# Transposing 256 tokens instead of all 1040 before the first projections of a hybrid attention and convolution block

## The chip, the core and the metric

The kernel is one program on one core of a Trainium2 chip. Its time is the device time of one execution in microseconds (us), and a lower time is better. Of the engines, PE multiplies matrices (PEld is its loading of weights), DVE is the vector engine, ACT the scalar engine, POOL the general one, and SP issues most of the loads and stores (DMA). Each engine works through its own list of instructions in order: where an instruction waits, all that is behind it on that engine waits too. SBUF is the on-chip memory, PSUM the banks into which PE adds up its products.

## The reference, cut to what is computed

```python
n = _rms(h, norm_mix_w[l])                 # h: 1040 tokens (16 meta, 1024 positions) x 1024 features
z = n @ w_in[l]                            # 7168 columns
q, k, v, glu, g_att, g_conv = jnp.split(z, splits, axis=-1)
o = _diff_attention(q, k, v, lam, cid)     # 8 heads, two maps each, block-causal
y_att = (_rms(o, subln_w[l]) * (1.0 - lambda_init)).reshape(b, lp, ATT_V)
u = glu[..., :CONV_CH] * jax.nn.sigmoid(glu[..., CONV_CH:])
u = jax.nn.silu(_layernorm(_causal_dwconv(u, ...), ...))      # 31 taps
m = jax.nn.sigmoid(g_att) * y_att + jax.nn.sigmoid(g_conv) * (u @ w_conv_out[l])
h = h + m @ w_out[l]
up = _causal_dwconv(_rms(h, norm_ffn_w[l]) @ w_up[l], ...)    # 3 taps
h = h + (silu(gate) * val) @ w_down[l]
out = _rms(h, norm_final_w)
```

`_rms(x, w)` divides each token by the root of its mean square over the 1024 features and multiplies by `w`. The matrix products are float32, made of three products of two rounded parts each (`hi hi`, `lo hi`, `hi lo`).

## The kernel before, in words

The products want the features on the 128 partitions: `xh` and `xl`, [128, 8 feature tiles, 1040 tokens], hold the two parts of the normalised tokens. The input comes in both layouts, `x` by tokens and `xT` feature-major, but the start of the kernel reads `x` alone. In three groups of 384, 384 and 272 tokens (the loop over `gi`), tiles `xt` of 128 tokens are loaded; ACT squares each with a sum along the row (L213), POOL turns the sum into a root (L214, L215), DVE scales the tile by it (L216), PE transposes it feature tile by feature tile into a pair of PSUM banks `ps_x` (L222), ACT writes `xh` from there (L225) and DVE `xl` (L226). 18 products `warm` of ones (L186) run on PE before the first tokens are there.

A weight's column tile [128, 1024] is loaded one use ahead and parted by ACT and DVE (`load_w`, L118 and L119). `mm3` (L143 to L145) is the three products of one feature tile; a "pass" below is the 24 products of one weight and one chunk of tokens.

Eight steps follow, one for each head (`inputs`). A step makes, for the three chunks of `CH_ALL`, the two halves of the gated unit (`ps_b`, through tanh on ACT into `tb`, then `ps_a`, which DVE multiplies into `u`, L278), then a gate (`ps_g`), the key (`ps_k`), the query (`ps_q`) and the value (`ps_v`); gate and query go by `CH_OUT`, chunks of 342. These use two PSUM banks in turn (`bank`). Step 0 makes the key of a chunk right behind its `ps_b` and `ps_a`. Beside the products of step i runs the attention of head i-1 (`attention`), a unit of work for each half pass, in the order of the table `UNITS`: `s` are scores, `v` turns the values, `t` turns the probabilities, `a` multiplies them with the values, and `n` (`norm`, L553 to L556) divides the outputs of the head before by their root mean square. Scores, `norm` and `ps_x` share two PSUM pairs (tag "s") in turn; `norm` holds its pair `ps_ss` until DVE has multiplied `os` by it (L556). A step begins with the units `s0 v0 n`, `s1`, (empty), `v1`, `s2`; so the pair that `norm` holds is the one that `s2` gets. The convolution runs on DVE with the lowest priority. The order on each engine is set by a scheduler that knows priorities and its own guess of durations, and then stands fixed in the program.

After the eight steps come the remaining gates, the merge and output projection, and a gated MLP; the change doesn't touch their code.

Of the kernel before, what the change touches and what calls it, by code (L numbers as in the profile page):

```python
# [19 lines left out]
KT = 8                # feature tiles of the model width  # L20
WARM = 18
T = 1040              # 16 meta tokens and 1024 positions
NM = 16               # meta tokens
T0 = 14               # first token whose residual stream is needed
TN = T - T0           # 1026
# [4 lines left out]
FT = 22               # feature tiles of the gate (and of the value)  # L30
LAMBDA_INIT = 0.2
CH_ALL = [(0, 348), (348, 346), (694, 346)]
CH_OUT = [(14, 342), (356, 342), (698, 342)]
NEG = -1e30
# A head's attention by units of work: v by tokens, scores, transposes, products with v, and the norm of the
# head before it.  A unit goes with half a bank of another product's passes.
# [15 lines left out]
LATE = 7                # the first head whose gate is computed after the last step  # L52
STATS_FROM, METAS_FROM = 8, 18          # units of the last head's attention
LATER = 1000            # what gives way: the convolution to the next step's work, a chunk's last scaling to the
                        # next chunk's sums
DIRECT = 2              # of w_up's tiles, pairs by plain products
W_LATER = 300           # the parts of a weight that is not used yet
GROUPS = [3, 4, 4]      # pairs of feature tiles that w_down's products sum over in PSUM
AHEAD, BEFORE = 5, 3    # steps whose parts are made ahead, and those of them before the last tile of w_up is done
# [3 lines left out]
def trunk_kernel(  # L63
    ctx: ExitStack,
    tc: tile.TileContext,
    x: bass.AP,         # [1040, 1024]     meta tokens and positions
    xT: bass.AP,        # [128, 8, 1040]   the same, feature-major
    w_in: bass.AP,      # [56, 128, 1024]  per column tile: [k within tile, (k tile, column)]
    w_co: bass.AP,      # [8, 128, 1024]
    w_o: bass.AP,       # [8, 128, 1024]  # L70
    w_up: bass.AP,      # [44, 128, 1024]
    w_dn: bass.AP,      # [22, 128, 1024]  rows of w_down
    lam4: bass.AP,      # [128, 4, 64]
    pvec: bass.AP,      # [128, 49]  norm_mix, norm_ffn, norm_final, ln_w, ln_b, dw_b (8 each), subln
    dww: bass.AP,       # [128, 8, 31]
    fdw: bass.AP,       # [128, 44, 3]
    fdb: bass.AP,       # [128, 44]
    out: bass.AP,       # [128, 8, 1024]
):
    nc = tc.nc  # L80
    # ------------------------------------------------------------ constants
# [28 lines left out]
    def load_w(src, later):  # L110
        """Column tile of a weight as its two float32r parts."""
        raw = wpool.tile([P, KT * P], F32, tag="wraw", name="wraw", bufs=2)
# [10 lines left out]
    class Weights:  # L123
        """The column tiles in the order of their use, each loaded one use ahead."""
# [4 lines left out]
        def ahead(self):  # L129
            if self.srcs:  # L130
                self.ready.append(load_w(self.srcs.pop(0), self.later))
# [9 lines left out]
    def mm3(ps, lh, ll, rh, rl, start, stop):  # L141
        """ps += l^T r from the two parts of each operand."""
        nc.tensor.matmul(ps, lh, rh, start=start, stop=False)  # L143
        nc.tensor.matmul(ps, lh, rl, start=False, stop=False)  # L144
        nc.tensor.matmul(ps, ll, rh, start=False, stop=stop)  # L145
# [13 lines left out]
    def rstd(dst, src, eps, n):  # L159
        """dst = (src / n + eps) ** -0.5"""  # L160
        nc.scalar.activation(dst, src, AF.Ln, bias=eps, scale=1.0 / n)
        nc.scalar.activation(dst, dst, AF.Exp, scale=-0.5)

    # =================================================== phase A: mixing inputs
# [18 lines left out]
    # ---- the tensor engine's clock rises while the first tokens arrive  # L183
# [4 lines left out]
    # ---- normalised tokens, transposed  # L188
# [8 lines left out]
    with tc.tile_pool(name="xp", bufs=2, reuse_waits="tile") as xp:  # L197
        rt = xp.tile([P, 9], F32, tag="rt", name="rt", bufs=1)
        nc.sync.dma_start(pv, pvec)
        for gi, (o, n) in enumerate(((0, 384), (384, 384), (768, 272))):  # L200
            tiles = []
            for t in range(o, o + n, P):
                r = min(P, T - t)
                xt = xp.tile([P, D], F32, tag="xt", name="xt", bufs=6)
                nc.sync.dma_start(xt[:r], x[t:t + r, :])
                tiles.append((t, r, xt))
            if gi == 0:
                for _ in range(3):
                    weights.ahead()
            for t, r, xt in tiles:  # L210
                c = rt[:r, t // P:t // P + 1]
                sq = xp.tile([P, D], F32, tag="sq", name="sq", bufs=2)
                nc.scalar.activation(sq[:r], xt[:r], AF.Square, accum_out=c)  # L213
                nc.gpsimd.tensor_scalar(c, c, 1.0 / D, 1e-6, op0=ALU.mult, op1=ALU.add)  # L214
                nc.gpsimd.tensor_tensor(out=c, in0=c, in1=half[:r], op=ALU.pow)  # L215
                nc.vector.tensor_scalar(xt[:r], xt[:r], c, None, op0=ALU.mult)  # L216
            for k in range(KT):
                if k % 2 == 0:
                    ps = ps_s.tile([P, 2, 512], F32, tag="s", name="ps_x")
                xn = ps[:, k % 2, :]  # L220
                for t, r, xt in tiles:
                    nc.tensor.transpose(xn[:, t - o:t - o + r], xt[:r, P * k:P * k + P], ident[:r, :r])  # L222
                xn = xn[:, :n]
                nw = pv[:, k:k + 1]
# [988 lines left out]
```

## Time and profile before

| | us |
|---|---|
| time, median of 3 runs | 1747.07 |
| lowest and highest | 1746.29, 1747.51 |
| span of the profiled execution | 1740.7 |
| until the first product of the gate of step 0 | 62.70 |
| PE busy in that stretch | 54.43 |
| PE busy from there to 740 | 677.30 of 677.30 |

The profiled execution has 1740.7 us from its first to its last instruction, 6.4 us less than the median time. In the profile a group of instructions is named by its line in the code, its engine, its operation and by "out<-in" with the names of tiles; "idle before" is what the engine waited ahead of it, and the arrow names what released it.

### The profile page before, as it was taken

To read this page: it belongs to the slowest core of one execution; us is meant where nothing else is said; L and a number is where in the kernel's file an instruction comes from. 1 tells how busy PE (TensorE), PEld (TensorE's weight loads), DVE (VectorE), ACT (ScalarE), POOL (GpSimd) and SP (SyncE) were. 2 spreads that over 40 slices of the span, in tenths; PEclk is the share of its full clock that TensorE was granted. 3 is DMA by queue.
4 is the path that set the end of the run, shared out by engine and by line. 5 is a ranking of instruction groups with operands and counts; after the bars stand their busy time and mean duration, and the time that the engine had idled before them with its cause. 6 is when DMAs were issued, how large, how long until landed. Compare 5 with 4: busy or idle time off the path is not lost.

```text
span 1740.7 us, 29030 instructions
## 1 busy us (share of the span) xinstructions
PE 1716.3 (99%) x11736; PEld 1651.5 (95%) x11736; DVE 1391.4 (80%) x2065; ACT 849.6 (49%) x1407; POOL 39.4 (2%) x75
## 2 busy tenths in 40 slices
PE   8999999999999999999999999999999999999997
PEld 6999999999999999998999999999999999988886
DVE  5679697978888797986357466998888888799997
ACT  6245565646464637565642245543334434353345
POOL 2020000000000000000000000000000000000010
PEclk9999999999999999999999999999999999999999
DMA  4323222141414141367648443322222221583622
GB/s 167 98 67 86 79 66 88 54 111 50 116 49 105 49 111 42 104 193 221 183 136 250 170 144 112 121 98 79 80 74 73 86 85 37 188 279 100 189 55 97
DMA packets 80710, 195.58 MB, mean 112 GB/s; under 512 B 8624, under 2 KB 26416, under 8 KB 80192
## 3 DMA queue, kind: packets, MB, share of 16 engines
q1 hardware_dynamic: 78416, 187.43, 33.8%
q0 software_dynamic: 2160, 6.29, 2.0%
q8 instruction: 92, 1.51, 0.4%
q14 instruction: 42, 0.34, 0.1%
HBM read 130.54 MB, written 40.93 MB: 99 GB/s over the span
## 4 chain that ended last, share of the span: by engine, by line
PE 89%; DMA 5%; DVE 3%; ACT 1%; issue 1%; SPq 0%; POOL 0%; DVEq 0%; ACTq 0%
PE ps_u L144 8%; PE ps_u L145 8%; PE ps_u L143 8%; PE ps_d L145 4%; PE ps_d L143 4%; PE ps_d L144 4%; PE ps_g L143 3%; PE ps_g L144 3%; PE ps_g L145 3%; PE ps_s L398 2%; PE ps_s L399 2%; PE pt L508 2%; PE ps_o L143 2%; PE ps_o L144 2%; PE ps_o L145 2%; PE ps_b L144 2%
## 5 line engine op out<-in xcount | busy, mean ns | idle before, releaser
L299 DVE SCALAR_TENSOR_TENSOR acc<-d,taps,acc 128x513 f32<-128x513 f32 x248 | 170.3, 746 | 0.5
L118 ACT CAST whi<-wraw 128x1024 fp32r<-128x1024 f32 x84 | 88.1, 1050 | 119.5 <-PE ps_o L144 31.4
L145 PE MATMUL ps_g<-xh,wlo 128*128 128x342 f32 x384 | 125.6, 327 | 0.0
L143 PE MATMUL ps_g<-xh,whi 128*128 128x342 f32 x384 | 124.9, 325 | 0.5 <-ACT tg L264 0.5
L143 PE MATMUL ps_d<-part 128*128 128x512 f32 (+1 forms) x324 | 123.9, 382 | 0.0
L144 PE MATMUL ps_d<-part 128*128 128x512 f32 (+1 forms) x324 | 122.8, 379 | 0.9 <-DVE part L981 0.9
L144 PE MATMUL ps_g<-xl,whi 128*128 128x342 f32 x384 | 123.7, 322 | 0.0
L145 PE MATMUL ps_d<-part 128*128 128x512 f32 (+1 forms) x324 | 123.4, 381 | 0.0
L926 DVE TENSOR_TENSOR u<-ps_u,u 128x516 f32<-128x516 f32 x140 | 94.7, 689 | 34.8 <-PE ps_u L145 34.3
L119 DVE TENSOR_TENSOR wlo<-wraw,whi 128x1024 fp32r<-128x1024 f32 x84 | 102.3, 1218 | 22.0 <-ACT whi L118 20.2
L1009 ACT CAST part<-raw 128x1024 fp32r<-128x1024 f32 x66 | 69.0, 1051 | 95.0 <-PE ps_d L145 73.9
L827 DVE SCALAR_TENSOR_TENSOR g<-u,fw,g 128x1024 f32<-128x1024 f32 x88 | 110.6, 1277 | 0.6
L299 DVE SCALAR_TENSOR_TENSOR acc<-u,tab,acc 128x513 f32<-128x513 f32 x120 | 88.5, 737 | 0.8
L981 DVE TENSOR_TENSOR part<-raw,part 128x1024 fp32r<-128x1024 f32 x66 | 80.0, 1218 | 5.0 <-ACT part L1009 4.4
L143 PEld LDWEIGHTS ps_g<-xh,whi 128*128 128x128 f32 x384 | 73.0, 190 | 1.2 <-ACT tg L264 0.8
L144 PEld LDWEIGHTS ps_d<-part 128*128 128x128 f32 x324 | 60.9, 188 | 13.6 <-DVE part L981 1.4
L143 PE MATMUL ps_o<-mmh,whi 128*128 128x258 f32 x256 | 72.5, 283 | 1.0 <-DVE sg L744 1.0
L145 PEld LDWEIGHTS ps_g<-xh,wlo 128*128 128x128 f32 x384 | 72.9, 190 | 0.3
L144 PEld LDWEIGHTS ps_g<-xl,whi 128*128 128x128 f32 x384 | 72.7, 189 | 0.4
L398 PE MATMUL ps_s<-kh,q 128*128 128x392 f32 (+5 forms) x224 | 72.7, 333 | 0.0
L145 PEld LDWEIGHTS ps_d<-part 128*128 128x128 f32 x324 | 60.8, 188 | 12.2
L144 PE MATMUL ps_o<-mml,whi 128*128 128x258 f32 x256 | 72.3, 283 | 0.0
(323 smaller groups left out, 6039.0 us busy)
## 6 DMA issues: line engine op xcount, KB each, us to landing
wraw<-in_w_in_dram SPq DMA_DIRECT2D x56, 512.0 KB, 3.4
wraw<-in_w_up_dram SPq DMA_DIRECT2D x44, 512.0 KB, 3.3
a_d<-g SPq DMA_DIRECT2D x22, 512.0 KB, 3.0
raw<-in_w_dn_dram SPq DMA_DIRECT2D x22, 512.0 KB, 6.5
raw<-a_d SPq DMA_DIRECT2D x22, 512.0 KB, 7.3
lnc<-conv_d SPq DMA_DIRECT2D x16, 513.0 KB, 4.1
wraw<-in_w_o_dram SPq DMA_DIRECT2D x16, 512.0 KB, 3.7
kh<-kh SPq DMA_DIRECT2D x24, 260.0 KB, 3.8
```

What stands on the lines that cost most here:

```text
L118: nc.scalar.copy(hi, rv)
L119: nc.vector.tensor_tensor(out=lo, in0=rv, in1=hi.bitcast(F32), op=ALU.subtract)
L143: nc.tensor.matmul(ps, lh, rh, start=start, stop=False)
L144: nc.tensor.matmul(ps, lh, rl, start=False, stop=False)
L145: nc.tensor.matmul(ps, ll, rh, start=False, stop=stop)
L299: nc.vector.scalar_tensor_tensor(out=out, in0=src[:, k:k + n], scalar=w, in1=add, op0=ALU.mult, op1=ALU.add)
L398: nc.tensor.matmul(ps, qs, kh[m][:, k0:k0 + n], start=True, stop=False)
L399: nc.tensor.matmul(ps, qs, kl[m][:, k0:k0 + n], start=False, stop=True)
L827: nc.vector.scalar_tensor_tensor(out=g, in0=u[:, :, 2 + k:2 + k + 512], scalar=fw[:, ct, k:k + 1], in1=g, op0=ALU.mult, op1=ALU.add)
L926: nc.vector.tensor_tensor(out=dst, in0=ps, in1=src, op=ALU.add)
L981: nc.vector.tensor_tensor(out=out, in0=x, in1=y, op=op)
L1009: nc.scalar.copy(hi, x)
```

## The change

Only the first 256 tokens go the old way, with their squares summed by DVE in one instruction for each tile (`tensor_tensor_reduce`). The other two chunks, now of 384 and 400 tokens, are read from `xT` feature-major, two feature tiles at a time, into tiles whose places later belong to the attention. Their tokens are still read by tokens too, for the squares and roots alone. For each tile of 128 tokens POOL makes a diagonal matrix of roots (`dg`), and PE multiplies ones by it, which spreads a row of roots over all partitions (`ps_r`). DVE multiplies each feature tile by the norm's weight and that row, ACT casts `xh`, DVE subtracts `xl`. `CH_ALL` becomes (256, 384, 400) for all eight steps. The third weight is loaded into a place of its own. Comments went too.

```diff
-CH_ALL = [(0, 348), (348, 346), (694, 346)]
+CH_ALL = [(0, 256), (256, 384), (640, 400)]
...
-        for gi, (o, n) in enumerate(((0, 384), (384, 384), (768, 272))):
+        def tokens_of(o, n):
             tiles = []
...
-                xt = xp.tile([P, D], F32, tag="xt", name="xt", bufs=6)
+                xt = xp.tile([P, D], F32, tag="xt", name="xt", bufs=5)
...
-            if gi == 0:
-                for _ in range(3):
-                    weights.ahead()
+            return tiles
+        def roots(tiles):
             for t, r, xt in tiles:
                 c = rt[:r, t // P:t // P + 1]
-                sq = xp.tile([P, D], F32, tag="sq", name="sq", bufs=2)
-                nc.scalar.activation(sq[:r], xt[:r], AF.Square, accum_out=c)
-                nc.gpsimd.tensor_scalar(c, c, 1.0 / D, 1e-6, op0=ALU.mult, op1=ALU.add)
+                sq = xp.tile([P, D], F32, tag="sq", name="sq", bufs=1)
+                if t < CH_ALL[0][1]:
+                    nc.vector.tensor_tensor_reduce(sq, xt, xt, 1.0 / D, 1e-6, ALU.mult, ALU.add, c)
+                else:
+                    nc.scalar.activation(sq[:r], xt[:r], AF.Square, scale=D ** -0.5, accum_out=c)
+                    nc.gpsimd.tensor_scalar(c, c, 1e-6, None, op0=ALU.add)
                 nc.gpsimd.tensor_tensor(out=c, in0=c, in1=half[:r], op=ALU.pow)
...
+        o, n = CH_ALL[0]
+        tiles = tokens_of(o, n)
+        for _ in range(2):
+            weights.ahead()
...
+        for gi, (o, n) in enumerate(CH_ALL[1:]):
+            tiles = tokens_of(o, n)
+            if gi == 0:
+                weights.ahead(xp.tile([P, KT * P], F32, tag="wr", name="wraw", bufs=1))
+            xf = []
+            for k, tag in zip(range(0, KT, 2), (("os", "sqh", "sql", "vh"), ("vl", "acc", "qt", "q0"))[gi]):
+                t = sp.tile([P, 2, n], F32, tag=tag, name="xf", bufs=1)
+                nc.sync.dma_start(t, xT[:, k:k + 2, o:o + n])
+                xf += [t[:, 0], t[:, 1]]
+            rb = ps_s.tile([P, 2, 512], F32, tag="s", name="ps_r")[:, 0, :n]
+            for t, r, xt, c in roots(tiles):
+                dg = xp.tile([P, P], F32, tag="dg", name="dg", bufs=2)
+                nc.gpsimd.tensor_scalar(dg[:r, :r], ident[:r, :r], c, None, op0=ALU.mult)
+                nc.tensor.matmul(rb[:, t - o:t - o + r], ones[:r], dg[:r, :r], start=True, stop=True)
+            for k, c in enumerate(xf):
+                nc.vector.scalar_tensor_tensor(out=c, in0=c, scalar=pv[:, k:k + 1], in1=rb, op0=ALU.mult, op1=ALU.mult)
+                hi = xh[:, k, o:o + n]
+                nc.scalar.copy(hi, c)
+                nc.vector.tensor_tensor(out=xl[:, k, o:o + n], in0=c, in1=hi.bitcast(F32), op=ALU.subtract)
```

The first place where the order matters is ACT at the end of the first chunk of step 0. Before, it alternates squares of coming tokens (L213) with `xh` of the second group (L225):

```order
L225 ACTIVATE xh<-ps_x,pv 128x384 [waits PE_49]
L274 ACTIVATE tb<-ps_b 128x348 [waits PE_49]
L225 ACTIVATE xh<-ps_x,pv 128x384 [waits DVE_49,PE_49]
L213 ACTIVATE sq,rt<-xt 128x1024 [waits DMAHW0_49,Activation_49]
L225 ACTIVATE xh<-ps_x,pv 128x384 [waits PE_49] x2
```

Now the casts of the second chunk (L261) and the squares of the third chunk's tokens (L219) stand in one row, and the third of these squares comes behind the seventh cast:

```order
L261 CAST xh<-xf 128x384 [waits DMAHW1_49,DVE_49]
L309 ACTIVATE tb<-ps_b 128x256 [waits PE_49]
L261 CAST xh<-xf 128x384 [waits DVE_49]
L261 CAST xh<-xf 128x384 [waits DMAHW2_49,DVE_49]
L219 ACTIVATE sq,rt<-xt 128x1024 [waits DMAHW5_49,Activation_49]
L261 CAST xh<-xf 128x384 [waits DVE_49]
L219 ACTIVATE sq,rt<-xt 128x1024 [waits DMAHW6_49,Activation_49]
L261 CAST xh<-xf 128x384 [waits DMAHW3_49,DVE_49]
L261 CAST xh<-xf 128x384 [waits DVE_49]
L261 CAST xh<-xf 128x384 [waits DMAHW4_49,DVE_49]
L219 ACTIVATE sq,rt<-xt 128x1024 [waits DMAHW7_49,Activation_49]
```

The second place is PE at the same point, now: the root spreading of the third chunk's tokens (L257) stands between the last key product of the first chunk and the first product of the second chunk (before, there is a transposition or nothing between such passes):

```order
L146 MATMUL ps_k<-xh,wlo 128x256
L257 MATMUL ps_r<-dg,ones 128x128 [waits Pool_49] x2
L144 MATMUL ps_b<-xh,whi 128x384 [waits DVE_49]
L145 MATMUL ps_b<-xl,whi 128x384
L146 MATMUL ps_b<-xh,wlo 128x384
```

The third place is PE early in step 2, where head 1 is attended to; the same stands in steps 3 to 7, with other score widths in step 7. Before, the unit `v1` (`ps_vt`) is followed by half of the second chunk's pass `ps_b`, and then by the first score of the unit `s2`, the one that gets the pair of `norm`:

```order
L421 MATMUL ps_vt<-ident,vt 128x128 x3
L143 MATMUL ps_b<-xh,whi 128x346 [waits Activation_49]
L144 MATMUL ps_b<-xl,whi 128x346
L145 MATMUL ps_b<-xh,wlo 128x346
L143 MATMUL ps_b<-xh,whi 128x346
```

Now the two scores of the first map stand ahead of that half pass:

```order
L456 MATMUL ps_vt<-ident,vt 128x128 [waits DVE_49]
L456 MATMUL ps_vt<-ident,vt 128x128 x3
L433 MATMUL ps_s<-kh_1654,q_1756 128x400 [waits DVE_49,PE_49]
L434 MATMUL ps_s<-kl_1656,q_1756 128x400
L144 MATMUL ps_b<-xh,whi 128x384 [waits Activation_49]
L145 MATMUL ps_b<-xl,whi 128x384
```

What moved is `s2`: from 12 products behind `v1` to right behind it. The chain of `norm` on ACT and DVE (L161, L162, L556 before; L162, L163, L591 now) has the same order as before.

## Rows read from the trace of the kernel before

**Rows 1.** PE by stretches: start:end, length, busy (instructions), granted clock, DMA share, GB/s
```profile
0.00:62.70 62.70, 54.43 (x325) 0.95 0.35 126
62.70:740.00 677.30, 677.30 (x4467) 1.00 0.28 81
```

**Rows 2.** PE's waits over the whole span: total us, times, longest
```profile
PE ps_x L222 <- DVE xt L216: 4.2, 3, 2.8
PE ps_x L222 <- DVE xl L226: 2.5, 3, 1.4
```

**Rows 3.** Timeline of ACT at the start: start, length, instruction, idle before
```profile
5.49 1.06 ACT L213 ACTIVATE sq<-xt 128x1024 f32<-128x1024 f32 x1 [3.06 <-DMA xt<-in_x_dram]
6.46 0.19 ACT L213 ACTIVATION_READ_ACCUMULATOR sq<-xt 128x1 f32 x1
...
9.49 1.05 ACT L118 CAST whi<-wraw 128x1024 fp32r<-128x1024 f32 x1
...
35.09 0.45 ACT L319 CAST kh<-ps_k 128x348 fp32r<-128x348 f32 x1 [1.33 <-PE ps_k L145]
```

**Rows 4.** Groups until 62.70 us, by shape: busy, mean ns of one, idle before
```profile
L226 DVE SCALAR_TENSOR_TENSOR xl<-ps_x,pv,xh 128x384 fp32r<-128x384 f32 x16 | 9.4, 610 | 0.6 <-ACT xh L225 0.4
L225 ACT ACTIVATE xh<-ps_x,pv 128x272 fp32r<-128x272 f32 x8 | 3.9, 489 | 4.4 <-PE ps_x L222 4.4
```

**Rows 5.** Timeline of PE: the first product, and a whole pass of 346 columns, products of 256 and 400
```profile
13.11 0.66 PE L143 MATMUL ps_b<-xh,whi 128*128 128x348 f32 x1 [0.46 <-ACT xh L225]
...
51.27 0.32 PE L143 MATMUL ps_b<-xh,whi 128*128 128x346 f32 x1
...
55.07 0.32 PE L143 MATMUL ps_a<-xh,whi 128*128 128x346 f32 x1
...
98.75 0.28 PE L398 MATMUL ps_s<-kh,q 128*128 128x256 f32 x1
98.87 0.28 PE L399 MATMUL ps_s<-kl,q 128*128 128x256 f32 x1
...
200.38 0.35 PE L398 MATMUL ps_s<-kh,q 128*128 128x400 f32 x1
200.57 0.34 PE L399 MATMUL ps_s<-kl,q 128*128 128x400 f32 x1
```

**Rows 6.** Timeline of POOL at the start
```profile
9.74 0.75 POOL L214 TENSOR_SCALAR rt<-rt 128x1 f32<-128x1 f32 x1
10.57 0.55 POOL L215 TENSOR_TENSOR rt<-rt,half 128x1 f32<-128x1 f32 x1
15.60 0.19 POOL L214 TENSOR_SCALAR rt<-rt 128x1 f32<-128x1 f32 x1 [4.48 <-ACT sq L213]
```

**Rows 7.** PE by stretches of a microsecond or less, columns as in Rows 1
```profile
31.00:32.00 1.00, 0.00 (x0) 1.00 0.00 0
...
812.00:813.00 1.00, 0.00 (x0) 1.00 0.29 115
...
816.50:817.00 0.50, 0.50 (x5) 0.74 0.00 0
817.00:818.00 1.00, 1.00 (x5) 0.50 0.09 16
...
820.00:821.00 1.00, 1.00 (x9) 0.93 0.86 338
```

**Rows 8.** Timeline early in step 2, all engines
```profile
189.98 0.28 PE L398 MATMUL ps_s<-kh,q 128*128 128x256 f32 x1
...
191.09 0.59 ACT L428 CAST vh<-ps_vt 128x512 fp32r<-128x512 f32 x1 [1.22 <-PE ps_vt L421]
...
196.46 1.01 ACT L162 ACTIVATE ps_ss<-ps_ss 128x1024 f32<-128x1024 f32 x1
...
197.50 1.22 DVE L556 TENSOR_TENSOR os<-os,ps_ss 128x1024 f32<-128x1024 f32 x1 [1.80 <-ACT ps_ss L162]
...
198.40 0.40 PE L143 MATMUL ps_b<-xh,whi 128*128 128x346 f32 x1
```

More of the change, by code (lines that the diff above doesn't have):

```diff
@@ L108, in trunk_kernel, with load_w @@
     nc.scalar.activation(lnw, eps6, AF.Exp)
-    def load_w(src, later):
-        raw = wpool.tile([P, KT * P], F32, tag="wraw", name="wraw", bufs=2)
+    def load_w(src, later, raw=None):
+        if raw is None:
+            raw = wpool.tile([P, KT * P], F32, tag="wraw", name="wraw", bufs=2)
         nc.sync.dma_start(raw, src)
@@ L127, in __init__, with ahead @@
             self.srcs, self.ready, self.later = list(srcs), [], W_LATER
-        def ahead(self):
+        def ahead(self, raw=None):
             if self.srcs:
-                self.ready.append(load_w(self.srcs.pop(0), self.later))
+                self.ready.append(load_w(self.srcs.pop(0), self.later, raw))
         def __call__(self):
@@ L203, in trunk_kernel @@
                 r = min(P, T - t)
-                xt = xp.tile([P, D], F32, tag="xt", name="xt", bufs=6)
+                xt = xp.tile([P, D], F32, tag="xt", name="xt", bufs=5)
                 nc.sync.dma_start(xt[:r], x[t:t + r, :])
                 tiles.append((t, r, xt))
-            if gi == 0:
-                for _ in range(3):
-                    weights.ahead()
+            return tiles
+        def roots(tiles):
             for t, r, xt in tiles:
                 c = rt[:r, t // P:t // P + 1]
-                sq = xp.tile([P, D], F32, tag="sq", name="sq", bufs=2)
-                nc.scalar.activation(sq[:r], xt[:r], AF.Square, accum_out=c)
-                nc.gpsimd.tensor_scalar(c, c, 1.0 / D, 1e-6, op0=ALU.mult, op1=ALU.add)
-                nc.gpsimd.tensor_tensor(out=c, in0=c, in1=half[:r], op=ALU.pow)
-                nc.vector.tensor_scalar(xt[:r], xt[:r], c, None, op0=ALU.mult)
@@ L217, in trunk_kernel @@
[L217 to L224, printed above, removed]
-                nc.scalar.activation(xh[:, k, o:o + n], xn, AF.Copy, scale=nw)
-                nc.vector.scalar_tensor_tensor(out=xl[:, k, o:o + n], in0=xn, scalar=nw,
-                                               in1=xh[:, k, o:o + n].bitcast(F32), op0=ALU.mult, op1=ALU.subtract)
+                sq = xp.tile([P, D], F32, tag="sq", name="sq", bufs=1)
@@ new lines, in roots @@
+                if t < CH_ALL[0][1]:
[3 more added lines that the diff above has]
+                    nc.gpsimd.tensor_scalar(c, c, 1e-6, None, op0=ALU.add)
+                nc.gpsimd.tensor_tensor(out=c, in0=c, in1=half[:r], op=ALU.pow)
+                yield t, r, xt, c
+        o, n = CH_ALL[0]
+        tiles = tokens_of(o, n)
@@ new lines, in trunk_kernel @@
+        for _ in range(2):
+            weights.ahead()
+        for t, r, xt, c in roots(tiles):
+            nc.vector.tensor_scalar(xt[:r], xt[:r], c, None, op0=ALU.mult)
+        for k in range(KT):
+            if k % 2 == 0:
+                ps = ps_s.tile([P, 2, 512], F32, tag="s", name="ps_x")
+            xn = ps[:, k % 2, :]
+            for t, r, xt in tiles:
+                nc.tensor.transpose(xn[:, t - o:t - o + r], xt[:r, P * k:P * k + P], ident[:r, :r])
+            xn = xn[:, :n]
+            nw = pv[:, k:k + 1]
+            nc.scalar.activation(xh[:, k, o:o + n], xn, AF.Copy, scale=nw)
+            nc.vector.scalar_tensor_tensor(out=xl[:, k, o:o + n], in0=xn, scalar=nw,
+                                           in1=xh[:, k, o:o + n].bitcast(F32), op0=ALU.mult, op1=ALU.subtract)
@@ new lines, in trunk_kernel @@
+        for gi, (o, n) in enumerate(CH_ALL[1:]):
[8 more added lines that the diff above has]
+            rb = ps_s.tile([P, 2, 512], F32, tag="s", name="ps_r")[:, 0, :n]
+            for t, r, xt, c in roots(tiles):
+                dg = xp.tile([P, P], F32, tag="dg", name="dg", bufs=2)
[6 more added lines that the diff above has]
+                nc.vector.tensor_tensor(out=xl[:, k, o:o + n], in0=c, in1=hi.bitcast(F32), op=ALU.subtract)
@@ L262, in gate @@
             yield from projg(ps[:, :n], w, xh, xl, o, n)
-            tg = xnp.tile([P, 348], F32, tag="tanh", name="tg", bufs=2)[:, :n]
+            tg = xnp.tile([P, 400], F32, tag="tanh", name="tg", bufs=2)[:, :n]
             nc.scalar.activation(tg, ps[:, :n], AF.Tanh, scale=0.5)
@@ L272, in glu @@
         yield from projg(ps[:, :n], wb, xh, xl, o, n)
-        tb = xnp.tile([P, 348], F32, tag="tanh", name="tb", bufs=2)
+        tb = xnp.tile([P, 400], F32, tag="tanh", name="tb", bufs=2)
         nc.scalar.activation(tb[:, :n], ps[:, :n], AF.Tanh, scale=0.5)
```

## Prediction

> **What bounds the kernel now.** I read the stretches of PE first. From the first product of step 0's gate at 62.70 us to 740, PE is busy for the whole 677.30 us; until 62.70 it is busy for 54.43 [rows 1]. So what lengthens PE's work, or makes it wait, in the eight steps costs in full, and what shortens the start can gain at most what lies idle or slow there. The list of PE's waits names the start: 4.2 us for the scaled tokens and 2.5 us for the split of the transposed ones [rows 2], besides the wait ahead of the first product at 13.11 us [rows 5]. In the steps the list has no wait at all. But a wait that isn't there now can have little room, so I then read the place where the order changed most, the head's beginning with the unit `norm` in step 2 [rows 8].
>
> **What a product costs by its width.** A pass of 24 products of 346 columns takes 55.07 - 51.27 = 3.80 us, 0.158 each; products of 256 columns follow one another by 0.12 us, those of 400 by 0.19 [rows 5]. That is near enough a straight line (0.46 ns a column), so three chunks of 256, 384 and 400 cost what 348, 346 and 346 cost: 72 x (0.120 + 0.176 + 0.185) = 34.6 us against 72 x 3 x 0.158 = 34.1. I take no change from the widths alone. What changes is when a chunk is over: a pass over the first chunk is 24 x 0.038 = 0.9 us shorter.
>
> **The start, step by step.** DVE's sum of squares isn't in the trace before. Its bounds come from a DVE instruction with two tensors of 384 columns, 0.61 us [rows 4]: no less than that, and by columns 1.63 for 1024. ACT's square with its sum takes 1.06 + 0.19 [rows 3]; I take 1.3, near that row of the same width, and half a microsecond either way for each of the two tiles. The first tile is there at 5.49 [rows 3], so the two tiles are squared by 8.2, scaled by some 9.8 and transposed by 10.4. ACT casts two weights ahead of its first `xh`; the first of these casts began at 9.49 [rows 3], behind three squares that ACT no longer has, and with two tiles of tokens ahead of the weights rather than three, the second weight now comes in the place of the first. So I have ACT done with both at about 10.55. With 0.47 for an `xh` of 256 columns (0.49 for 272 [rows 4]) PE starts at 11.1, 2 us earlier than now.
>
> From there ACT sets the pace of the first chunk: eight `xh` (3.8), three squares of the second chunk's tokens (3.75) and the third weight (1.05), 8.6 us in all, end at 19.2. The last `xl` and three diagonal products on PE follow, and DVE can begin the second chunk at about 21.2. Each feature tile needs two DVE instructions (about 0.6 and 0.5) and a cast (0.45, as for 348 columns [rows 3]). By the order, the third square of the third chunk's tokens comes behind seven casts, a tanh and two squares: 7 x 0.45 + 0.45 + 3 x 1.25 = 7.35 us of ACT from 21.8 on, to 29.2. POOL then needs three instructions for the diagonal (0.19 and 0.55 [rows 6], and a wider one, which I put at 0.3), PE a float32 product of 128 columns (0.3, as an estimate, a little over two products of 256 columns at 0.12): 30.6, and with four hand-overs 31.1. PE has these diagonal products ahead of the second chunk's first product. By its own work it would be through the first chunk, the key included, at about 27, so it stands with hardly any work for some 4 us. **This wait takes the place of the ones removed.** The second and third chunk are 72 x 0.176 + 72 x 0.185 + 0.3 = 26.3 us, with DVE and ACT ahead of PE by then (DVE ends the third chunk's tiles near 42 and PE needs its last tokens after 44): 57.4.
>
> The granted clock falls to half after such a pause: after the pause at 812 it stood at 0.50, from about 816.7 (0.74 in the half microsecond up to 817) to 820.1 (0.93 in the one after 820); but at 31 to 32 a whole microsecond without PE left it at 1.00 [rows 7]. The new pause is rather of the longer kind. At half clock for 3.4 us, 1.7 us of work are lost. I take it: **59.1 instead of 62.70, a gain of 3.6 us** (5.3 without the fall). What the gate's weights need is loaded and cast beside the third chunk.
>
> [...] The trace shows a POOL instruction of 0.19 us taking 0.75 beside DVE's scaling [rows 6]; for two SBUF inputs, as the new subtractions have, no row shows it. With POOL's three instructions held once each by 0.5 us, the pause would be 1.5 us longer and the sum 1.5 us higher; I leave it out, since DVE mostly has an operand in PSUM or waits when POOL's last diagonal is due.
>
> **The eight steps.** Here the order has moved `s2`. In step 2 now, `s0` starts on PE at 189.98; the values are turned, `norm`'s sums made; then ACT goes through the scores' exponentials and a logarithm and an exponential over `ps_ss`, the last at 196.46, and DVE multiplies by `ps_ss` from 197.50 to 198.72 [rows 8], 8.74 us after `s0` began. Only then is the pair free, and `s2` takes that pair. In the trace `s2` runs at 200.38 [rows 5], 1.7 us after that: nobody waits. In the changed order PE comes to it right behind `v1`, where the second chunk's pass starts now (198.40 [rows 8]), 8.42 us after `s0`. And it comes there faster, for 36 products of the first chunk lie between: 36 x 0.038 = 1.37, so 7.05 us after `s0`. ACT's chain doesn't get faster with the chunk, for it starts from `ps_vt` and waits for nothing of the pass (ACT had idled 1.22 us ahead of it [rows 8]). PE waits 8.74 - 7.05 + 0.06 for the hand-over, 1.75 us, and the half pass behind, which doesn't need the pair, waits with it. Only 2 of the 4 scores are moved, but PE's order is fixed. Steps 2 to 7 all begin with `norm` (step 1 has no head before it) and all have this order, with a narrower score in step 7. So the **loss is 6 x 1.75 = 10.5 us**. PE has no other wait in these steps that it could shorten, so nothing gives it back. Chunks two and three are wider, so units beside them get more room; the first chunk's key and value passes have only waits with some tenths of room left by my reading, which I price at nothing.
>
> Bounds: if ACT's exponentials start up to 0.15 us later, for DVE is then still at the head's last part, a wait is 1.9 (11.4 in all). If the scheduler's order hands the pair over sooner than the trace lets me see, it is 1.4 (8.4).
>
> **Sum.** 1740.7 - 3.6 + 10.5 = 1747.6 for the span, and with the 6.4 us that lie outside it 1754.0; the same from the median, 1747.07 + 6.9. A measurement of this kernel can tell a change of about 0.2%, 3.5 us, from none.
>
> **Rivals.**
> *The pause at the second chunk doesn't happen* (ACT's squares and casts are shorter, or the scheduler's order is kinder than I read it): PE runs through from 27, step 0's gate starts at 27 + 26.3 = 53.3, a gain of 9.4, and with the six waits the time is 1748.2: no change. For it: the plan of the change needs it, and DVE and ACT idle much of the start now. Against: the row of casts and squares on ACT is nearly without holes by my sum.
> *The six waits don't come, and it is faster.* They come from `norm`'s multiplication being the last reader of the pair; were `s2` to get the pair of `s0`, which is free long before, there would be none, and the start's gain stands alone: 1743.5, or 1737.7 without the pause. It decides at once: with less than 0 left of the 1.75 us in each step. Against it: the wait on DVE stands on the moved score, and two pairs in turn give it that one.
> *Each of the six waits also halves the clock.* 1.75 us is near the 1.4 us pause at 31 that left the clock alone [rows 2, 7], but not far from the pause at 812 that didn't. Each fall costs 1.7 us more: 1754.0 + 10.2 = 1764.2.
>
> **How the numbers follow.** The forecast, a shorter start and six waits, has 0.60: with gains of 1.5 to 5.3 and losses of 8.4 to 11.4 it spans 1750.7 to 1757.0. No pause has 0.17, no waits 0.12, falling clock 0.11. The predicted time is the forecast's, 1754. The range of 1744 to 1759 holds the forecast and the no-pause case, and leaves out the falling clock and most of the faster case. Faster by over 0.2% (under 1743.6) is the case without waits, 0.12; within 0.2% the one without a pause, 0.17; slower the forecast and the falling clock, 0.71.
>
> **What would show it.** In the list of PE's waits, a row of scores waiting for DVE's `os`, six times and some 1.7 us each, in steps 2 to 7; without it the loss is wrong. At the start, a pause of PE ahead of the second chunk, released by POOL's diagonal, with ACT busy up to it; PE's first product at about 11; the first gate product near 59, or 57 if the granted clock stays. If the clock falls behind the six waits, the stretches behind them show 0.50. If the first chunk's squares on DVE last over 2 us, the start's gain is smaller by as much.

## The result, and the profile after

The changed kernel takes 1761.99 us (median of 4 runs, 1761.14 to 1763.32) where the kernel before takes 1746.68 beside it: a ratio of 1.0081, interval 1.0068 to 1.0094. It is slower, as forecast, but by 15.3 us where 7 were forecast, and above the range. Timed again on another chip the ratio was 1.0086 (1.0069 to 1.0102).

The profiled execution has a span of 1759.5 us, 18.8 more than the one before. (Its median lies 2.5 us above its profile's span, the other's 6, so the medians are less far apart than the profiles.) Here is where the 18.8 us lie. First PE by the two stretches of [rows 1], the boundary now at the first product of step 0's gate (columns as there):

```profile
0.00:58.93 58.93, 49.49 (x282) 0.91 0.53 190
58.93:740.00 681.07, 670.62 (x4402) 1.00 0.28 80
```

PE reaches the gate 3.77 us earlier than in [rows 1], and in the steps, where it never stood still, it now stands for 10.5. Its list of waits after, the same view as [rows 2], names what for:

```profile
PE ps_s L433 <- DVE os L591: 10.3, 6, 1.7
PE ps_r L257 <- POOL dg L256: 4.2, 4, 1.5
PE ps_x L236 <- DVE xt L230: 2.8, 2, 2.0
...
PE ps_x L236 <- DVE xl L240: 1.0, 1, 1.0
```

Then the marks on PE's timeline: the first product, the second chunk, step 0's gate, the first gate of the last head's stage (behind step 7), and the first product of the MLP's `ps_u`:

```profile
10.82 0.58 PE L144 MATMUL ps_b<-xh,whi 128*128 128x256 f32 x1 [0.46 <-ACT xh L239]
...
31.06 0.49 PE L144 MATMUL ps_b<-xh,whi 128*128 128x384 f32 x1
...
58.93 0.32 PE L144 MATMUL ps_g<-xh,whi 128*128 128x342 f32 x1
...
741.95 0.31 PE L144 MATMUL ps_g<-xh,whi 128*128 128x342 f32 x1
...
1078.04 0.28 PE L144 MATMUL ps_u<-b11h,whi 128*128 128x258 f32 x1
```

and the last two of them in the kernel before:

```profile
731.99 0.32 PE L143 MATMUL ps_g<-xh,whi 128*128 128x342 f32 x1
...
1059.33 0.28 PE L143 MATMUL ps_u<-b11h,whi 128*128 128x258 f32 x1
```

| stretch | before | after | difference | forecast |
|---|---|---|---|---|
| to step 0's gate | 62.70 | 58.93 | -3.8 | -3.6 |
| from there to the last head's stage | 669.29 | 683.02 | +13.7 | +10.5 |
| last head's stage and merge, to the MLP | 327.34 | 336.09 | +8.7 | none |
| the MLP | 681.4 | 681.5 | 0.1 | none |

The first term was right, the second too small, and a third had no line in the sum. (By the medians, the third is some 5 us, as an estimate: 15.3 + 3.8 - 13.7.) I call that third one, from the first gate product behind step 7 to the first product of `ps_u`, **the late stretch**. The experiments ask three things: whether the new widths alone make the waits, whether the pause in the start is what I took it for, and what lengthens the late stretch, whose instructions are the same as before.

### The profile page after: what moved, and what is told of

The parts are those of the page before. It is cut to its first block, busy times and chain, and to the rows that moved or that the text cites. A ratio compares the mean times of both kernels' runs of the same rounds, so it can differ in the third digit from the quotient of the medians.

```text
span 1759.5 us, 28973 instructions
## 1 busy us (share of the span) xinstructions
PE 1718.5 (98%) x11694; PEld 1649.6 (94%) x11694; DVE 1397.3 (79%) x2078; ACT 846.0 (48%) x1403; POOL 39.3 (2%) x80
## 4 chain that ended last, share of the span: by engine, by line
PE 84%; DMA 6%; DVE 4%; ACT 4%; issue 1%; SPq 0%; POOL 0%; DVEq 0%; ACTq 0%; POOLq 0%
PE ps_u L145 8%; PE ps_u L146 8%; PE ps_u L144 8%; PE ps_d L146 4%; PE ps_d L144 4%; PE ps_d L145 4%; PE ps_g L144 2%; PE ps_g L146 2%; PE ps_g L145 2%; PE ps_s L433 2%; PE pt L543 2%; DMA ma<-matt_d 2%; PE ps_s L434 2%; PE ps_o L144 2%; PE ps_o L145 2%; PE ps_o L146 2%
## 5 line engine op out<-in xcount | busy, mean ns | idle before, releaser
L433 PE MATMUL ps_s<-kh,q 128*128 128x392 f32 (+5 forms) x224 | 74.6, 342 | 11.1 <-DVE os L591 10.3
L145 PEld LDWEIGHTS ps_d<-part 128*128 128x128 f32 x324 | 60.9, 188 | 13.5 <-DVE part L1016 1.2
L146 PE MATMUL ps_o<-mmh,wlo 128*128 128x258 f32 x256 | 72.3, 283 | 0.0
```

What stands on the lines that cost most here:

```text
L433: nc.tensor.matmul(ps, qs, kh[m][:, k0:k0 + n], start=True, stop=False)
```

## The experiments

Ratios are to the kernel before, run on the same chip, with 95% intervals.

**Widths and start apart.** Steps 1 to 7 got the old chunks back and kept the new start:

```diff
+CH_OLD = [(0, 348), (348, 346), (694, 346)]
...
+    def chunks(i):
+        return CH_OLD if i else CH_ALL
...
-        for o, n in CH_ALL:
+        for o, n in chunks(i):
```

> The changed kernel with its new start, but steps 1 to 7 take chunks of 348, 346 and 346 again (step 0 keeps 256, 384 and 400). Theory: all that was lost sits in the order that the new widths give to steps 2 to 7 and to the last head behind them (six waits of a score for the pair of norm, and loads of convolved rows that stand behind a weight). So no score waits for os, DVE doesn't stand 3.5 us for a convolved row, the gate of step 0 starts at 58.9, and the time is 1747 - 3.8 = 1743. Rival 1, the last head loses because everything comes at other moments than before and loads collide: its 8.7 us stay, 1752. Rival 2, wider products cost more than their columns: the part of the loss beyond the listed waits (0.6 us a step) goes, but this can't be told from the theory here; the run with the old start does that.

The six waits are gone: between 90 and 728 us no wait of PE is listed, and the kernel reaches the last head's stage 3.5 us ahead of before, just as it left the start. But the ratio is 0.9999 (0.9986 to 1.0012), and the late stretch measured 330.4 us. The widths make the waits; something that comes with the start, and not with the order of the last head (which is as before here), takes its gain back.

The reverse, the old start with the new widths, `CH_ALL = [(0, 256), (256, 384), (640, 400)]` in the kernel before and its tanh tiles 400 wide:

> The kernel before with its old start (all tokens transposed in groups of 384, 384 and 272, squares on ACT), and only CH_ALL set to 256, 384 and 400 in all steps (with it the two tanh tiles, 400 wide as in the changed kernel). Theory: the widths alone bring the six waits, 6 x 2.3 = 13.8 us with the small gaps around them, and the last head's 8.7: 1747 + 22.5 = 1769.5, give or take 2 for the start, whose first chunk is shorter. Rival, the new start is what disturbs the last head: 1747 + 13.8 = 1761. Second rival, the widths are harmless and the waits come with the new start: 1747.

1.0084 (1.0064 to 1.0104). PE waits 10.4 us for `os`, six times, and the steps take 12.7 us more. The late stretch has the order of the changed kernel, yet takes 330.6, 3.3 more than in the first profile of before and not 8.7. So half of my theory fell: that order alone doesn't cost 8.7.

Step 7 alone with old widths (`CH_OLD if i == 7 else CH_ALL`), which brings back the last head's old order:

> The changed kernel, but step 7 alone takes chunks of 348, 346 and 346. Theory: the order around the last head (SP's loads of convolved rows and of weights, PE's gates and scores) depends on the widths of step 7 and is as before now: five waits for os are left in steps 2 to 6, the one in step 7 goes (2.3 us), and the 8.7 us behind step 7 go: 1762 - 11 = 1751. Rival, those 8.7 us come from the moments at which things happen and not from the order: 1762 - 2.3 = 1759.7.

1.0067 (1.0049 to 1.0084). Five waits for `os` are left (8.6 us), and the late stretch is 331.5, between the theory's 327.3 and the rival's 336. By the ratio, 11.7 us above before, the rival's number (13) lies in the interval and the theory's (4) doesn't: the old order of the last head alone doesn't give the 8.7 us back.

**Whose pair the score gets.** The word `n` goes one unit further back in both tables:

```diff
-    "s0 v0 n", "s1", "", "v1", "s2", ...
+    "s0 v0", "s1 n", "", "v1", "s2", ...
```

> The changed kernel with one word moved in the table of units: n (norm) stands behind s1 and no longer ahead of it, so that the pairs in turn give s2 the pair of s1, and norm's pair goes to s3. Theory: the six waits come from norm being the last user of the pair that s2 gets, so no score waits for os any more, and the time is 1762 - 10.3 = 1751.7, or 1749 if the small gaps around the waits go too; the last head's loss stays. Rival, DVE and ACT are simply late at that place, whatever the pair: PE waits there as long as now, for something else, 1762.

1.0026 (1.0015 to 1.0037), by the ratios 9.6 us less than the changed kernel. PE's list of waits over the steps (90 to 730 us):

```profile
PE ps_s L433 <- DVE os L591: 1.3, 1, 1.3
```

Five of six are gone with no change to any width or engine's work; the one left is in step 7, whose table puts `s3` right behind `v1`. The two maps of `s3` take a pair each, and the second one gets `norm`'s. The mechanism of the six waits is settled: `norm` is the last user of the pair that the moved score is given.

**The pause in the start.** DVE's product into `u` for the first chunk of step 0 gets a higher priority:

```diff
+        tc.cur_priority -= early
         nc.vector.scalar_tensor_tensor(
             out=u[:, Z + o:Z + o + n], in0=tb[:, :n], ...)
+        tc.cur_priority += early
...
+                yield from glu(u, wb, wa, o, n, 500 if o == 0 else 0)
```

> The changed kernel, but DVE's product into u for the first chunk of step 0 gets a higher priority, so that it stands right behind the third xf of the second chunk and no longer behind all eight (three of its xf and two of its xl are ahead of the place it had). Theory of the pause: PE can't begin the second chunk's gated unit before DVE has emptied the bank into u, and the roots of the third chunk's tokens stand ahead of it only because of this; so PE begins the second chunk at about 24 to 27 in place of 31.1 and goes through it in DVE's pace of 1.2 us a feature tile, ends it near 40 in place of 45.8, and step 0's gate begins between 53.5 and 55.5 in place of 58.9: 1758. Rival, ACT's squares set the pace anyway (they are in the same row as the casts): the gate begins at 58 or later, 1762.

PE begins the second chunk at 26.71 and step 0's gate at 57.06: 1.9 us gained where I wanted 3.5 to 5.5. PE's waits between 20 and 60 us:

```profile
PE ps_r L257 <- POOL dg L256: 3.1, 3, 1.6
PE ps_b L144 <- DVE u L314: 1.6, 1, 1.6
```

The early `u` let the second chunk begin, but the roots of the third chunk's tokens still stop PE in it (1.58 at 29.32), and one chunk later the same pattern comes back: `u` of the second chunk stands behind the third chunk's `xf` (1.57 at 43.86). The time's ratio, 1.0075 (1.0058 to 1.0092), isn't apart from the changed kernel's. With the old widths as well, both repairs at once:

> Both repairs: steps 1 to 7 with chunks of 348, 346 and 346, and the early u of the first chunk. Against the run with the old steps alone, theory: 4 us less, 1739, 4.5 below the kernel before. Rival, the start's gain doesn't reach the end (the last head's stage takes back what comes earlier, as it took 3 us in the run with the old steps): 1743, no difference from before.

0.9990 (0.9981 to 0.9999), and 0.9989 (0.9977 to 1.0000) in a second timing: some 2 us faster than before, where the last head's stage is reached 5.8 us earlier. Again 3 to 4 us are given back in the late stretch (332.8 and 332.1).

**What the late stretch depends on.** First, does it repeat?

> The kernel before, once more, for a second profile. From the first gate product of the last head's stage to the first product of the MLP it took 327.3 us in the first profile, and 330.4 to 337.1 in the five kernels since. Theory: this stretch varies by its loads from execution to execution, so the second profile of the same kernel can lie some 3 us higher, 327 to 331. Rival: the stretch belongs to the kernel's order and start, and comes out at 327.3 within 0.5.

> The changed kernel, once more. The same stretch took 336.1 us in its first profile. Theory (it varies from execution to execution, and the changed order of the loads adds 2 to 4 us to its middle): 331 to 337. Rival (it belongs to the order): 336.1 within 0.5. Up to the last head's stage both say the same: step 0's gate at 58.9, six waits of 1.7 us.

Before: 329.7. After: 336.1. It varies by 2 us between executions, and it does belong to the kernel. In the changed kernel one loss comes at the same place in both of these profiles. The rows of SP and DVE, with SP's loads of convolved rows `lnc` and of a weight:

```profile
757.91 0.38 SPq L114 DMA_DIRECT2D wraw<-in_w_in_dram  x1
758.87 1.23 DVE L632 TENSOR_TENSOR st<-lnc 128x1026 f32<-128x1026 f32 x1
760.13 0.32 SPq L625 DMA_DIRECT2D lnc<-conv_d  x1
...
763.05 5.74 SPq L625 DMA_DIRECT2D lnc<-conv_d  x2
767.22 1.23 DVE L632 TENSOR_TENSOR st<-st,lnc 128x1026 f32<-128x1026 f32 x1 [3.52 <-DMA lnc<-conv_d]
```

and at the same place in the kernel before:

```profile
749.80 0.32 SPq L590 DMA_DIRECT2D lnc<-conv_d  x1
...
751.13 0.38 SPq L590 DMA_DIRECT2D lnc<-conv_d  x1
751.61 0.45 SPq L113 DMA_DIRECT2D wraw<-in_w_in_dram  x1
...
754.13 1.23 DVE L597 TENSOR_TENSOR st<-st,lnc 128x1026 f32<-128x1026 f32 x1 [1.52 <-DMA lnc<-conv_d]
```

Before, two rows and then the weight go out; after, the weight goes first, the row behind it takes 7.1 us from its issue to DVE's use where it took 4.3, and all that DVE has to do for PE's attention stands behind the waiting `st`. PE then stands twice (0.81 and 0.86 us), and its clock falls from 1.00 to 0.50; stretches of a microsecond in the changed kernel:

```profile
772.00:773.00 1.00, 0.90 (x3) 0.50 0.01 4
773.00:774.00 1.00, 1.00 (x5) 0.50 0.71 115
```

That is where the order can show: up to the convolution's mean PE took 49.2 and 49.0 us in these two profiles, 46.3 and 46.6 before. But the old start with this order took 46.4 there. Over all the profiles of this document, the eight with the new order lie between 46.4 and 49.2 (mean 47.5), the nine with the old one between 46.3 and 47.1 (46.5). So the order is worth about 1 us here, and nearly 3 only in the two profiles whose clock fell. Further on, at the merge, the kernels fall into two groups that have nothing to do with the order. Everything that PE waits for from 870 to 900 us in the second profile of the changed kernel:

```profile
PE ps_co L145 <- DVE cl L724: 0.8, 1, 0.8
PE ps_co L144 <- ACT ch L723: 0.8, 1, 0.8
```

With the old start there is only one such wait, of 0.5 to 0.6 (three profiles), and six of the seven profiles with the new start show 0.84 for `cl`. The wait for `ch` is 0.3 in the first profile of the changed kernel. The chain behind `ch` hangs on a load (`c<-conv_d`) that goes out together with a weight and a store. DMA over 8 us around it, in the kernel before and then in the second profile of the changed one (queue: packets, MB, share of 16 engines; then the issues with KB and us to landing):

```profile
q1 hardware_dynamic: 576, 1.40, 56.7%
issues: line engine op xcount, KB each, median us to landing
c<-conv_d SPq DMA_DIRECT2D x1, 513.0 KB, 5.4
```

```profile
q1 hardware_dynamic: 576, 1.40, 56.1%
q8 instruction: 1, 0.02, 0.7%
issues: line engine op xcount, KB each, median us to landing
c<-conv_d SPq DMA_DIRECT2D x1, 513.0 KB, 6.7
```

The same 576 packets, and one of "instruction" more. By the page of the profile that queue moves 92 packets of 16 KB in an execution. PE's 11694 products and as many weight loads make 254 instructions to a packet, so I took them for **PE's code**, a piece every 19 us on average (92 in 1759.5), 21 to 23 around the merge, which the profile counts on the same 16 engines as the data. No row says whose code a packet holds; the next runs ask whether its place costs time. The new start has 42 products fewer, with 42 weight loads (11736 of each on the page of before, 11694 on that of after), so by this reading all later pieces fall 84 instructions further on in the program. That can be tried with no order changed at all: small products in a corner of the warm-up bank, while PE waits for its first tokens.

```diff
+    for _ in range(21):
+        nc.tensor.matmul(warm[0:2, 0:2], ones[:, 0:2], ones[:, 0:2], start=True, stop=True)
```

On the kernel with both repairs:

> The kernel with both repairs (old widths in steps 1 to 7, early u) and 21 products of 2 columns by 2 into a corner of the warm-up bank, right behind the warm-up, where PE waits for tokens for 2 us; their results are used by nobody, and every engine's order is otherwise the same. Each is four of PE's instructions, 84 in all, as many as the new start has fewer than the old. Theory: PE's code comes in pieces of 16 KB over the same 16 DMA engines as the data, one piece every 22 us; in the kernels with the new start a piece falls 4 to 6 us ahead of the merge's first product, among a weight, a convolved row and a store for which ACT and DVE wait, in those with the old start 12 to 14 us ahead of it. With 84 instructions more it falls there again, the stretch from the last head's first gate to the MLP's first product goes from 332.8 back to 327.3 to 329.7, and the time is 1744.3 - 5.9 = 1738.5 where before is 1744.3. Rival, the pieces are too small to matter (one engine of 16 for 1 us): the stretch stays above 330.4 and the time is 1742 to 1743.

0.9965 (0.9953 to 0.9978), 5 to 6 us faster than before. In the same view as above, the piece has left the place, and the row lands in time (5.2 us; the line is the median of two rows that go out in these 8 us):

```profile
q1 hardware_dynamic: 576, 1.40, 54.9%
issues: line engine op xcount, KB each, median us to landing
c<-conv_d SPq DMA_DIRECT2D x2, 513.0 KB, 4.9
```

Against chance, both kernels again on one chip:

> Both repairs without the small products, timed beside the next run on the same chip. By the first pair (0.9990 and 0.9965 of before, on two chips) the place of PE's code is worth 4 us here: this run 1 to 3 us below before. If the first pair was chance, both runs lie at the same time, 3 to 5 below before.

> Both repairs with the 21 small products behind the warm-up, once more. Theory: 5 to 7 us below before and 3 to 5 below the run beside it. Rival (chance): the same time as the run beside it.

0.9989 (0.9977 to 1.0000) without and 0.9968 (0.9958 to 0.9978) with the small products, 3 us apart. It repeats, on the lower edge of what I expected. Both kernels reach the last head's stage at 726.28, so nothing of it lies in the start, where the small products are. Of the 4.9 and 3.8 us between the profiled spans of the two pairs, 3.9 and 2.3 lie in the late stretch and 1.3 and 1.5 in the MLP. The other way round, 43 small products in the kernel before (the same line with 43), to bring its pieces where the new start has them. On the pages of the two kernels with both repairs, 21 small products count as 42 products and 42 weight loads (11694 and 11736 of each), so 43 make 172 instructions; the 84 that the new start lacks and these 172 are together about one piece, by the 254 to a packet:

> The kernel before, with 43 of these small products behind the warm-up, where PE waits for tokens for 6 us; nothing else changes its place. [...] Theory: the stretch from the last head's first gate to the MLP grows from 327.3 and 329.7 to 330.4 or more, and the time by 2 to 4 us. Rival: no change, within 1 us of before.

1.0016 (1.0007 to 1.0025): slower by 2.8 us, though its start was 1.5 us shorter in the profile. The page of this profile counts 93 packets of "instruction" where all the other kernels have 92, which fits PE's code, longer here by those 172. Its late stretch is 330.0, hardly longer than in the second profile of before, and the profiled execution was 2.7 us faster than this kernel's median: where the 2.8 us lie isn't shown. In the changed kernel itself:

> The changed kernel with 21 of the small products behind the warm-up. Theory: PE's pieces of code fall where they did in the kernel before; the last head's stretch, 336.1 us twice, comes down by 3 to 6 us, and the time to some 1757; six waits for os and the start stay. Rival: 336 and 1762 as they are (the stretch is long because of the changed order of its loads alone).

1.0077 (1.0061 to 1.0092), the late stretch 327.8. The clock's fall at 772 is gone and so is the wait for `ch`; but 1.0077 isn't apart from the changed kernel's ratio. Both timed side by side:

> The changed kernel, timed beside the next one on the same chip. Theory (the place of PE's pieces of code costs it 6 us and more in the last head's stretch): 16 to 18 us above before, stretch 336. Rival (the profile with the shorter stretch was chance): the same distance as the next run, 12 to 13, stretch anywhere between 328 and 336.

> The changed kernel with the 21 small products behind the warm-up once more. Theory: 11 to 13 us above before, at least 4 below the run beside it, stretch 327.8 to 330. Rival: no difference from the run beside it.

1.0086 (1.0069 to 1.0102) without and 1.0073 (1.0057 to 1.0090) with; the profiles' late stretch 334.9 and 331.9. The profiles differ as expected, the times by only 1.4 us with intervals that overlap: for the changed kernel itself the expected 4 us and more aren't shown.

All profiles together, the late stretch by the two suspects; "far" is a piece some 12 to 14 us ahead of the merge's first product, "near" one some 4 to 6:

| | piece far | piece near |
|---|---|---|
| old order of the last head | 327.3, 329.7, 328.9, 329.8 | 330.0, 330.4, 331.5, 332.8, 332.1 |
| new order of the last head | 330.6, 327.8, 331.9 | 336.1, 336.1, 334.9, 337.1, 330.1 |

The means are 328.9 and 331.4 in the first line, 330.1 and 334.9 in the second. Each number is one execution: the 330.1 at the end is the early `u`, profiled in an execution 3.7 us faster than its median, and the 337.1 is the moved `norm`, profiled 4.9 us slower than its own. The waits at the merge follow the piece more closely. The row behind `ch` took 5.2 to 5.5 us to land in all seven profiles with the piece far, and 5.4 to 7.8 in the ten with it near, 6.0 or more in six. PE waits for `ch` in eight of those ten (0.13 to 2.05 us) and in none of the seven.

What the lengthening consists of can be read off every profile in the same way. The late stretch and the falls of the clock in it, before and then in the changed kernel (PE, columns as in [rows 1]):

```profile
731.99:1059.33 327.34, 321.50 (x2246) 0.99 0.59 186
815.00:822.00 7.00, 7.00 (x37) 0.76 0.69 217
```

```profile
741.95:1078.04 336.09, 325.45 (x2246) 0.98 0.60 181
771.00:777.00 6.00, 5.14 (x24) 0.72 0.63 202
829.00:838.00 9.00, 9.00 (x44) 0.62 0.67 182
```

Before, PE stands for 5.8 us of the stretch (327.34 - 321.50), and half clock costs 1.7 (7 x 0.24). In the changed kernel it is 10.6 and 5.1 (6 x 0.28 + 9 x 0.38). So the 8.7 us are 4.8 of standing, 3.4 of clock and 0.5 of anything else. In all 17 profiles, the stretch less its standing and less the cost of half clock is 319.3 to 320.5 us: orders and pieces of code lengthen it only in these two ways. The means of the table's four places, in its order, are 6.8, 8.5, 7.4 and 9.7 us of standing and 2.6, 3.1, 2.8 and 5.1 of clock.

## Why the prediction came out as it did

**The start was right, step by step.** PE's first product at 10.82 (forecast 11.1); DVE's sum of squares 1.22 us and 0.08 (1.3); the pause ahead of the second chunk, with ACT's third square read out by 29.04 (29.2), released by POOL's diagonal at 30.82, and the second chunk at 31.06 (31.1); the clock at half behind it:

```profile
31.00:32.00 1.00, 1.00 (x6) 0.64 0.03 12
32.00:33.00 1.00, 1.00 (x4) 0.50 0.00 0
33.00:34.00 1.00, 1.00 (x4) 0.50 0.02 8
34.00:35.00 1.00, 1.00 (x5) 0.66 0.03 8
35.00:36.00 1.00, 1.00 (x8) 1.00 0.00 0
```

That is 1.7 us lost, as forecast, and step 0's gate at 58.93 (59.1). POOL was slowed once in this pause: one diagonal took 1.27 us from 27.82 on, beside three of DVE's subtractions, which have two SBUF inputs, where five others took 0.62. (At 8.09 a root took 1.00 beside DVE's scaling, where others took 0.57. Beside DVE's `xl`, with an operand in PSUM, POOL's 0.19 and 0.55 at 17.63 and 17.90 in the kernel before were as long as at 29.87 and 30.14, with DVE idle.) The third square was read out only as it ended, so the pause wasn't longer for it; leaving it out of the sum was right.

**The six waits were right in place, cause and length** (1.72 us each, forecast 1.75), **but not in price.** The rows of step 2 that answer to [rows 8]:

```profile
185.98 0.28 PE L433 MATMUL ps_s<-kh,q 128*128 128x256 f32 x1
...
186.46 0.60 PE L456 MATMUL ps_vt<-ident,vt 128*128 128x128 f32 x4
...
186.82 0.48 PE L588 MATMUL ps_ss<-sqh,ones_r 128*128 128x512 f32 x1
...
192.56 0.60 PE L456 MATMUL ps_vt<-ident,vt 128*128 128x128 f32 x4
193.50 1.22 DVE L591 TENSOR_TENSOR os<-os,ps_ss 128x1024 f32<-128x1024 f32 x1 [1.95 <-ACT ps_ss L163]
...
194.87 0.42 PE L433 MATMUL ps_s<-kh,q 128*128 128x400 f32 x1 [1.72 <-DVE os L591]
```

Four turnings at 186.46 are followed 0.36 us later by the next product. Those at 192.56 are followed after 2.31, so the wait takes 1.95 of PE's time, 0.23 more than its listed idle time: at 186.82 the next product begins 0.24 us before the four turnings end (186.46 + 0.60), while behind those at 192.56 the idle time is counted only from their end, 193.15. The rest, to the 2.3 us by which each of these steps grew, lies in gaps of a tenth or two at other places where two tiles change hands. The widths themselves cost nothing, as the prediction took it: in the profile after, products of 256, 384 and 400 columns follow one another by 0.118, 0.175 and 0.183 us, 0.476 together, and three of 346 or 348 before by 0.477. The term should have been 13.8 (6 x 2.3) where the sum has 10.5. I sized it by the wait alone, and its bounds (8.4 to 11.4) were bounds of the wait.

**The step that failed is the sum's silence on what follows step 7.** I treated code that the diff doesn't touch as time that doesn't change, and the late stretch took 8.7 us more: 10.6 us of standing for 5.8 and 5.1 us lost to half clock for 1.7. Two things reached it, by the table above: its means grow by 1.2 us with the new order alone, by 2.5 with the new place of the code alone, and by 6 with both. The new widths of step 7 moved a weight ahead of a convolved row in SP's queue; the order of SP shows it, and the prediction speaks of the engines' orders alone. And the new start's smaller number of PE instructions moved the pieces of code against the program (the one ahead of the merge's first product lies 4 to 6 us ahead of it, no longer 12 to 14), of which the prediction has nothing. How the 8.7 us of this kernel divide between the two stays open. [Rows 7] could have warned: PE stands at 812, and its clock falls from 816.7 to 820, in this stretch already before. To its 5.8 us of standing and 1.7 of half clock the moved loads and code then added 4.8 and 3.4. The sum had a zero there, and the range no width for it. (One bound is also misadded, without effect: by its own terms the forecast spans 1750.2 to 1757.0, not 1750.7.)

Of the rivals, the one with no pause at the second chunk didn't come, and no clock fell behind the six waits: between 36 and 740 us the granted clock stood at 1.00 in every microsecond, so 1.7 us of standing left it alone six times, while in the last head two stops of less than 1 us each, 2 us apart, were followed by half clock in two profiles of three. The case without the six waits needed other widths in steps 1 to 7 (0.9999) or, but for one of them, another place for `norm` (1.0026). Neither alone was faster than before: the late stretch took back what the start had gained.

**What stays open.** Which of the pieces of code costs most in the late stretch (18 fall in it before, 17 in the changed kernel) isn't told apart; the one ahead of the merge is the one whose effect can be read in a row. In the changed kernel the effect shows in the profiles but not clearly in its times, and that a piece holds up a row is read from which rows land late, not from a trace of the transfers one by one. And its clock fell at 772 in two of its three profiles only: in the third DVE stood 2.4 us for the same row instead of 3.5 and 3.2, PE's stops were 0.88 and 0.69 us, and the clock stayed.

The best version that came of it is the one with both repairs and the small products, 0.9965 and 0.9968 of before. PE in its profile, columns as in [rows 1], with the boundary at step 0's gate:

```profile
0.00:57.22 57.22, 48.67 (x324) 0.97 0.54 196
57.22:740.00 682.78, 682.78 (x4503) 1.00 0.29 82
```

The start's gain is kept, and the steps are again without a wait.

## What to carry to other kernels

When a table of widths is shared by a start and by everything behind it, change it for the start alone first: here the widths cost 14 us in places that had no need of them. When a scheduler sets the order, compare the orders of all queues, SP's too, over the whole program, and look in each moved row for the tile that it must wait for, above all where two buffers are used in turn: the user that holds one longest decides. And give code that isn't touched a term of its own if it waits on loads, for the same instructions in the same order took 2 to 8 us more or less there.

## What the runs showed of the hardware that I had not expected

- Instructions of PE that do nothing changed the time. 84 of them made a kernel 3 to 4 us faster (0.9990 to 0.9965, and 0.9989 to 0.9968), and 172 made another one 2.8 us slower (1.0016), with every other instruction in its place on its engine. I put it down to the moment at which PE's code comes, relative to the data, which no trace shows by itself. With a packet of "instruction" some 4 to 6 us ahead of the merge's first product, a row of 513 KB took 5.4 to 7.8 us to land (ten profiles), with one 12 to 14 us ahead 5.2 to 5.5 (seven). No wait of PE for code is listed; PE waited for data that landed late, 0.13 to 2.05 us for `ch` in eight of the ten.
- A wait of 1.72 us cost 1.95 us of PE's time, by the distance of the products' starts.
